# The last pair of neighbourhood attention heads asks for its scores amid its values' projection

## The chip, the cores and the metric

The kernel runs on one core of a Trainium2 chip. Its time is the device time of one execution in microseconds (us). TensorE (PE) does the matrix products and transposes, VectorE (DVE) and ScalarE (ACT) read its results from the eight PSUM banks and do the elementwise work, GpSimd (POOL) does some multiplications and copies, and SyncE (SP) issues most of the DMAs. The engines run side by side; each executes its own instructions strictly in the order in which they were written.

## The reference

Two encoder layers over 256 tokens and 16 meta tokens, with a model width of 2048. In each layer one projection feeds two groups of heads, gated linear attention (GLA) and neighbourhood attention (NA); their outputs, 16 blocks of 128 rows, go through one output projection. An MLP follows.

```
proj = jnp.einsum('bld,dp->blp', h, w_in)
gq, gk, gv, gr, glr, nq, nk, nv = jnp.split(proj, points, axis=-1)
y_gla = _gla_mixer(gq, gk, gv, gr, glr, gla_w_up, gla_b_up, gla_norm_w)
y_na = _na_mixer(nq, nk, nv, na_rel_bias).astype(h.dtype)
mix = jnp.einsum('blm,md->bld', jnp.concatenate([y_gla, y_na], axis=-1), w_out)
h = _layer_norm(DEEPNORM_ALPHA * h + mix, ln1_w, ln1_b)
```

NA has 16 heads of 64: a softmax over a window of the token grid with a learned bias, plus the meta tokens as keys. Only the first layer computes the meta tokens' own outputs.

```
s_loc = jnp.where(col_mask[:, :, None, :], s_loc + bias, -jnp.inf)
s_meta = jnp.einsum('bhnqd,bhmd->bhnqm', qb, km)
s = jnp.concatenate([s_loc.reshape(B, NA_HEADS, ncb, NA_QB, n_loc), s_meta], axis=-1)
p = jax.nn.softmax(s, axis=-1)
out = (jnp.einsum('bhnqrk,bhrnkd->bhnqd', p_loc, v_blk)
       + jnp.einsum('bhnqm,bhmd->bhnqd', p[..., n_loc:], vm))
```

## The kernel before

Each fp32 operand is split into a high and a low part (`wh`, `wl`; `x` likewise). A weight tile of 128x1024 is loaded by SyncE into one of three `raw` buffers (L192); ScalarE makes `wh` from it (L215) and VectorE `wl` (L216). So a load waits until the `wl` subtraction of the tile three before has been done. The tiles come in the order in which the matmuls use them, loaded some tiles ahead.

The NA heads are handled in pairs, 0 to 7. For each pair the projection (`by_m`) makes three blocks of columns: Q, K and V, here written Q7, K7, V7 for the last pair. A block is accumulated in one PSUM bank in two halves of 24 matmuls (L250, `eight`). `ev_na` takes a finished block out of its bank: for V that is a copy `nv` on ScalarE (L540), a copy `nr` of the meta columns on VectorE (L541), and two copies that complete `nr` on GpSimd (L544). When V is there, `ev_na` appends the generator `na_pair` to the list `fg`. Layer 0 has 272 columns (with the meta tokens); layer 1 has 256.

What a generator does between two `yield`s is one step. `pump` is called amid each block and at its end and runs one step of the first generator of `fg`; at the same places it may run steps of the GLA heads from `bg`, and a foreground step that was announced with `yield True` lets a waiting background step go on. The steps of a pair are:

1. the bias load `nb`, the output `na_out` of the pair two before (where more than one is due), the scores (L778, and L782 for the meta tokens in layer 0), and the softmax: adds `ns` (L787) and `nms` (L789), REDUCE (L754), the exps on ScalarE (L756), RECIPROCAL (L757), and the multiplications on GpSimd (L760), into `ns` and `npr`;
2. in layer 0, the softmax of the meta tokens (`nms`);
3. the stream transposes `nt` of the weights on VectorE (L799, L800);
4. `fetch` of the pair before (four DMAs `np` on SyncE, L826), the transposes of the values on TensorE (L805, L806, L808 for `nms`), their copies `v` (L811 on ScalarE, L812 on VectorE) and `npm` (L817), and the DMA `hop` (L819) that writes `nt` to memory, from where `fetch` will read it in another layout;
5. for pair 7 alone: `na_out(6)`, `fetch` of its own `np`, and `na_out(7)`, a step each.

`na_out` (L851, L858) multiplies `np` by `v` in two PSUM banks, and ScalarE and VectorE (L861, L862) take the result out as one block of `y`. There is one buffer for `np`.

After V7 comes the output projection `by_k`, over the 16 blocks of `y` two at a time: k = 0, 2, ..., 14. It accumulates four banks at once (L302 in layer 0; L312, `dense`, in layer 1), two from each of two pools. `mixed(k)` runs one `fg` step ahead of each k, and further ones if the blocks k and k + 1 aren't done; it also writes two additions `acc` (L424). Before the change, pair 7's steps fall so: scores at the end of V7, meta softmax at k=0, stream transposes at k=2, value transposes at k=4, `na_out(6)` at k=6, `fetch` at k=8, `na_out(7)` at k=10.

The order on each engine is that in which Python emits the instructions, with weight tiles ahead of their use and `issue_after` placing some DMAs behind named instructions. The pools pick the banks.

Of the kernel before, what the change touches and what calls it, by code (L numbers as in the profile page):

```python
# [58 lines left out]
class Trunk:  # L59
# [464 lines left out]
    def ev_na(self, j, ps):  # L524

        nc, m = self.nc, j % 3
        src = ps[:, :T].rearrange("p (r t w) -> p t r w", t=2, r=ROWS)
        if m == 0:
            t = self.a2.tile([P, L], F32, name="nq", tag="nq")
            nc.scalar.mul(t[:, NM:].rearrange("p (t r w) -> p t r w", t=2, r=ROWS), src, NAD ** -0.5)  # L530
            if self.full:
                nc.vector.tensor_scalar(t[:, :NM], ps[:, T:], NAD ** -0.5, None, ALU.mult)
            self.nqkv = [t]
            return
        if m == 1:
            t = self.a2.tile([P, 2, NKEY], F32, name="nk", tag="nk")
            own, rest = t[:, :, :P], t[:, :, P:]
        else:
            t = own, rest = self.nv[j // 3 % 2]
        nc.scalar.copy(own.rearrange("p t (r w) -> p t r w", r=ROWS), src)  # L540
        nc.vector.tensor_copy(rest[:, :, 32:NK2], ps[:, None, T:L].to_broadcast([P, 2, NM]))  # L541
        grid = lambda a: a.rearrange("p (r w) -> p r w", r=ROWS)
        for h, lo in ((0, 0), (1, 24)):
            nc.gpsimd.tensor_copy(grid(rest[:, h, :32]), grid(own[:, 1 - h, :])[:, :, lo:lo + 8])  # L544
        self.nqkv.append(t)
        if m == 2:
            self.y[8 + j // 3] = self.pair(self.yp, "y", 8 + j // 3)
            self.fg.append(self.na_pair(j // 3, *self.nqkv))
            self.wants[self.fg[-1]] = True

    def ev_r(self, c, ps):

# [206 lines left out]
            r = st[:, 2 * u:3 * u, None].to_broadcast(list(i.shape))  # L759
            by.tensor_tensor(o, i, r, ALU.mult)  # L760

    def na_pair(self, c, q, k, v):
        nc, b = self.nc, self.a2
        heads = [slice(hh * NAD, hh * NAD + NAD) for hh in range(2)]
        two = lambda a: a.rearrange("p (t c) -> p t c", t=2)
        bias = b.tile([P, 4, 192], F32, name="nb", tag="nb").rearrange("p u c -> p (u c)")[:, :4 * NKEY]
        bias = bias.rearrange("p (u c) -> p u c", u=4)
        nc.sync.dma_start(bias, self.i["nab"][self.l, c])
        s = b.tile([P, 4, NKEY], F32, name="ns", tag="ns", bufs=1)
        st = b.tile([P, 12], F32, name="nst", tag="nst")  # L770
        if len(self.due) > 1:
            self.due.popleft()()
        ps = self.spare(2)
        for t in range(2):
            for hh, hs in enumerate(heads):
                for part in heads:
                    at = NM + t * P + part.start
                    nc.tensor.matmul(ps[hh][part, t * NKEY:t * NKEY + NKEY], lhsT=q[hs, at:at + NAD], rhs=k[hs, t, :],  # L778
                                     start=True, stop=True)
        if self.full:  # L780
            for hh, hs in enumerate(heads):
                nc.tensor.matmul(ps[hh][:NAD, 2 * NKEY:2 * NKEY + NK2], lhsT=q[hs, :NAD], rhs=k[hs, 0, P:],  # L782
                                 start=True, stop=True)
            meta = self.nms
            sm = meta[:NM, :, :NK2]
        for hh in range(2):
            nc.vector.tensor_tensor(s[:, 2 * hh:2 * hh + 2, :], two(ps[hh][:, :2 * NKEY]), bias[:, 2 * hh:2 * hh + 2, :], ALU.add)  # L787
            if self.full:
                nc.vector.tensor_tensor(sm[:, hh, :], ps[hh][:NM, 2 * NKEY:2 * NKEY + NK2], self.qmask, ALU.add)  # L789
        pr = self.npr  # L790
        self.softmax(s, st, 4, ((s[:, :, :P], s[:, :, :P]), (pr[:, :, :NK2], s[:, :, P:])), nc.gpsimd)
        yield
        if self.full:
            mt = b.tile([NM, 6], F32, name="mst", tag="mst")
            self.softmax(sm, mt, 2, ((sm, sm),), nc.gpsimd)
        yield
        turned = b.tile([P, 4, 192], F32, name="nt", tag="nb")
        out = lambda at, n: turned[:, :, at:at + 32 * n].rearrange("p j (u c) -> p u j c", c=32)
        nc.vector.transpose(out(0, 4), s[:, :, :P])  # L799
        nc.vector.transpose(out(P, 2), pr.rearrange("p (h t) c -> p h (t c)", t=2))  # L800
        yield True
        self.fetch()
        pv = self.bank()
        for t in range(2):
            nc.tensor.transpose(pv[:, t * P:t * P + P], v[0][:, t, :], self.ident)  # L805
        nc.tensor.transpose(pv[:, T:T + P], v[1].rearrange("p t c -> p (t c)"), self.ident)  # L806
        if self.full:
            nc.tensor.transpose(pv[:, T + P:], meta.rearrange("p u c -> p (u c)"), self.ident)  # L808
        v1 = b.tile([P, 2, P], F32, name="v1", tag="v1")
        v2 = b.tile([P, P], F32, name="v2", tag="v2")  # L810
        nc.scalar.copy(v1, two(pv[:, :T]))  # L811
        nc.vector.tensor_copy(v2, pv[:, T:T + P])  # L812
        pm = None
        if self.full:
            pm = self.npm[c % 2]
            for hh, hs in enumerate(heads):
                nc.vector.tensor_copy(pm[hs, hh, :], pv[hs, T + P:T + P + NM])  # L817
        hop = self.hp.tile([P, 4, 192], F32, name="hop", tag="hop")
        nc.scalar.dma_start(hop, turned)  # L819
        p = []  # L820

        def fetch():
            p.append(b.tile([P, 4, 192], F32, name="np", tag="np", bufs=1))
            with self.tc.issue_after(self.asked):
                for j in range(4):
                    nc.sync.dma_start(p[0][32 * j:32 * j + 32], hop.rearrange("(i k) j c -> k i j c", i=4)[:, :, j])  # L826

        self.fetch = fetch
        self.due.append(lambda: self.na_out(c, v1, v2, p[0], pm))
        yield True  # L830
        if c == 7:
            self.due.popleft()()
            yield
            fetch()
            yield
            self.due.popleft()()
            yield
# [444 lines left out]
```

## Time and profile before

| | us |
|---|---|
| median of 3 runs | 2315.6 |
| the runs | 2315.4, 2315.6, 2317.69 |
| span of the profiled execution | 2314.3 |
| TensorE busy | 2300.4 |
| VectorE busy | 1519.4 |
| ScalarE busy | 1224.6 |
| GpSimd busy | 160.4 |

The profiled execution's own time is not listed apart from the runs; its span lies 1.3 us below their median, and 1.1 below the shortest of them. Times in the profile are microseconds from the span's start. The output projection begins at 331.8 in layer 0 and at 1505.0 in layer 1. A timeline row gives start, duration, engine, line, operation, output and inputs, shape, how many, and in brackets how long the engine stood idle before and what it was released by. A row of a TensorE wait gives what waited and for what, then the total, the number of times and the longest. The rows themselves are shown in the prediction.

### The profile page before, as it was taken

To read this page: it belongs to the slowest core of one execution; us is meant where nothing else is said; L and a number is where in the kernel's file an instruction comes from. 1 tells how busy PE (TensorE), PEld (TensorE's weight loads), DVE (VectorE), ACT (ScalarE), POOL (GpSimd) and SP (SyncE) were. 2 spreads that over 40 slices of the span, in tenths; PEclk is the share of its full clock that TensorE was granted. 3 is DMA by queue.
4 is the path that set the end of the run, shared out by engine and by line. 5 is a ranking of instruction groups with operands and counts; after the bars stand their busy time and mean duration, and the time that the engine had idled before them with its cause. 6 is when DMAs were issued, how large, how long until landed. Compare 5 with 4: busy or idle time off the path is not lost.

```text
span 2314.3 us, 45228 instructions
## 1 busy us (share of the span) xinstructions
PE 2300.4 (99%) x18420; PEld 2186.8 (94%) x18420; DVE 1519.4 (66%) x2392; ACT 1224.6 (53%) x2096; POOL 160.4 (7%) x245
## 2 busy tenths in 40 slices
PE   9999999999999999999999999999999999999998
PEld 9999999999999999999999899989988888888888
DVE  5588778875544455547576788788866455666654
ACT  5666665564433344444456766655654334555443
POOL 0023210100000000000020122200100000000000
PEclk9999999999999999999999999999999999999999
DMA  8556665555566666555555566666666666666664
GB/s 263 162 164 185 200 197 177 174 180 177 181 182 178 179 181 181 177 181 181 177 179 165 174 180 204 213 185 191 188 192 193 196 189 195 193 193 221 194 199 138
DMA packets 129824, 431.65 MB, mean 187 GB/s; under 512 B 14792, under 2 KB 23496, under 8 KB 129616
## 3 DMA queue, kind: packets, MB, share of 16 engines
q1 hardware_dynamic: 127024, 421.95, 60.1%
q10 hardware_dynamic: 2592, 6.82, 0.8%
q8 instruction: 144, 2.36, 0.4%
q14 instruction: 64, 0.52, 0.1%
HBM read 420.32 MB, written 8.39 MB: 185 GB/s over the span
## 4 chain that ended last, share of the span: by engine, by line
PE 79%; DVE 3%; ACT 1%; issue 1%; DMA 0%; POOL 0%; DVEq 0%; ACTq 0%; POOLq 0%; SPq 0%
PE mm L250 44%; PE mm L262 30%; PE mm L302 2%; PE mm L312 1%; DVE wl L216 1%; PE bg L312 0%; ACT wh L215 0%; PE bg L302 0%; DMA raw<-in_win 0%; DVE acc L1085 0%; PE bg L851 0%; DVE S L615 0%; ACT ns L756 0%; PE bg L983 0%; PE bg L470 0%
## 5 line engine op out<-in xcount | busy, mean ns | idle before, releaser
L216 DVE TENSOR_TENSOR wl<-raw,wh 128x1024 fp32r<-128x1024 f32 (+1 forms) x770 | 936.3, 1223 | 619.8 <-ACT wh L215 518.4
L215 ACT CAST wh<-raw 128x1024 fp32r<-128x1024 f32 (+1 forms) x770 | 805.4, 1048 | 753.2 <-PE mm L250 360.1
L250 PE MATMUL mm<-x,wh 128*128 128x272 f32 (+3 forms) x4544 | 805.3, 294 | 0.0
L250 PEld LDWEIGHTS mm<-x,wh 128*128 128x128 f32 x4544 | 646.8, 188 | 15.4 <-DVE gtn L577 0.3
L250 PE MATMUL mm<-x,wl 128*128 128x272 f32 (+3 forms) x2432 | 519.6, 284 | 0.0
L250 PEld LDWEIGHTS mm<-x,wl 128*128 128x128 f32 x2432 | 390.8, 188 | 0.0
L250 PE MATMUL mm<-y,wh 128*128 128x272 f32 (+1 forms) x1440 | 235.0, 285 | 0.0
L250 PEld LDWEIGHTS mm<-y,wh 128*128 128x128 f32 x1440 | 199.7, 188 | 0.1
L262 PE MATMUL mm<-x,wh 128*128 128x512 f32 x832 | 193.8, 390 | 0.0
L262 PEld LDWEIGHTS mm<-x,wh 128*128 128x128 f32 x832 | 154.3, 188 | 31.0
L250 PE MATMUL mm<-u,wh 128*128 128x272 f32 (+1 forms) x1056 | 172.1, 285 | 0.0
L262 PE MATMUL mm<-y,wh 128*128 128x512 f32 x688 | 162.2, 389 | 0.0
L262 PEld LDWEIGHTS mm<-y,wh 128*128 128x128 f32 x688 | 128.7, 188 | 26.5
L250 PE MATMUL mm<-y,wl 128*128 128x272 f32 (+1 forms) x720 | 146.4, 284 | 0.0
L250 PEld LDWEIGHTS mm<-u,wh 128*128 128x128 f32 x1056 | 146.3, 188 | 0.0
L262 PE MATMUL mm<-u,wh 128*128 128x512 f32 x496 | 118.3, 391 | 0.0
L250 PEld LDWEIGHTS mm<-y,wl 128*128 128x128 f32 x720 | 112.5, 188 | 0.0
L262 PEld LDWEIGHTS mm<-u,wh 128*128 128x128 f32 x496 | 90.9, 188 | 17.7
L250 PE MATMUL mm<-u,wl 128*128 128x272 f32 (+1 forms) x528 | 107.3, 284 | 0.0
L262 PEld LDWEIGHTS mm<-x,wl 128*128 128x128 f32 x832 | 98.4, 188 | 2.0
L262 PE MATMUL mm<-x,wl 128*128 128x256 f32 x832 | 98.8, 276 | 0.0
L262 PEld LDWEIGHTS mm<-y,wl 128*128 128x128 f32 x688 | 84.2, 188 | 2.8
(285 smaller groups left out, 2288.7 us busy)
## 6 DMA issues: line engine op xcount, KB each, us to landing
raw<-in_wff SPq DMA_DIRECT2D x512, 512.0 KB, 3.8
raw<-in_win SPq DMA_DIRECT2D x190, 512.0 KB, 4.3
raw<-in_wout SPq DMA_DIRECT2D x64, 512.0 KB, 4.2
hop<-nt ACTq DMA_DIRECT2D x16, 384.0 KB, 2.3
np<-hop SPq DMA_DIRECT2D x64, 96.0 KB, 4.6
nb<-in_nab SPq DMA_DIRECT2D x16, 352.0 KB, 4.9
xraw<-in_xT SPq DMA_DIRECT2D x7, 272.0 KB, 5.5
out<-out SPq DMA_DIRECT2D x5, 256.0 KB, 3.4
```

Source lines behind the costliest of these rows:

```text
L215: self.nc.scalar.copy(h, r)
L216: self.wl = self.nc.vector.tensor_tensor(lo, r, h.bitcast(F32), ALU.subtract).ins
L250: mm(o, lhsT=self.block(w, j), rhs=rhs, start=first and not i, stop=last and i == len(TURNS[once]) - 1)
L262: self.nc.tensor.matmul(o, lhsT=self.block(both[j // 8][low], j % 8), rhs=rhs, start=first and not i + j, stop=bool(last and i and j == 15 ...
L302: self.nc.tensor.matmul(ps[g + m][:, :n], lhsT=self.block(parts[p][0], 4 * j + m if first else 2 * m + j), rhs=acts[k + j][parts[p][1]][:, ...
L312: self.nc.tensor.matmul(o, lhsT=self.block(both[low], i), rhs=rhs, start=not low and k + i % 2 == 0, stop=k == DC - 2 and i % 2 == 1 and n ...
```

## The change

```diff
@@ ev_na @@
         if m == 2:
             self.y[8 + j // 3] = self.pair(self.yp, "y", 8 + j // 3)
-            self.fg.append(self.na_pair(j // 3, *self.nqkv))
-            self.wants[self.fg[-1]] = True
+        if m == (1 if j // 3 == 7 else 2):
+            self.fg.append(self.na_pair(j // 3, self.nqkv))
+            self.wants[self.fg[-1]] = m == 2
@@ na_pair @@
-    def na_pair(self, c, q, k, v):
-        nc, b = self.nc, self.a2
+    def na_pair(self, c, qkv):
+        nc, b, last = self.nc, self.a2, c == 7
+        q, k = qkv[:2]
+        if last:
+            yield True
...
         nc.vector.transpose(out(P, 2), pr.rearrange("p (h t) c -> p h (t c)", t=2))
+        if last:
+            yield
         yield True
         self.fetch()
+        v = qkv[2]
         pv = self.bank()
...
         yield True
-        if c == 7:
+        if last:
             self.due.popleft()()
             yield
             fetch()
```

Pair 7's generator is appended when K7 has been taken out of its bank, not V7. Its first step, at the end of K7, does nothing but wait for its turn. Its scores (with `na_out(5)` ahead of them) then come amid V7, its meta softmax at the end of V7, its stream transposes at k=0; the step at k=2 does nothing; and from the value transposes at k=4 on, the steps fall where they did. `v` is taken from the list when it is needed. This happens in both layers. No instruction is added or removed; below L547 lines move down by 1 to 7 (L760 becomes L761, L787 L791, L812 L819, L826 L833, L851 L858).

The order changes on all engines. GpSimd, layer 1, from the copies for K7 on (`nk` and `nr` are the pieces for K7 and V7, `ns` and `npr` the softmax's multiplications). Before:

```order
L544 COPY nk<-nk 128x32 x2
L544 COPY nr_16662<-nv_16661 128x32 x2
L760 TENSOR_TENSOR ns<-ns,nst 128x4x128
L760 TENSOR_TENSOR npr<-ns,nst 128x4x48
L1073 TENSOR_SCALAR acc<-acc,vec 128x256 x8
```

After:

```order
L544 COPY nk<-nk 128x32 x2
L761 TENSOR_TENSOR ns<-ns,nst 128x4x128
L761 TENSOR_TENSOR npr<-ns,nst 128x4x48
L544 COPY nr_16662<-nv_16661 128x32 x2
L1080 TENSOR_SCALAR acc<-acc,vec 128x256 x8
```

The copies that complete `nr` now stand behind the multiplications of the softmax. In layer 0 it is the same, with `nms` behind `nr`.

VectorE, layer 1, from pair 7's REDUCE or RECIPROCAL to the copy `v`. Before:

```order
L754 TENSOR_REDUCE nst<-ns 128x4
L424 TENSOR_TENSOR acc<-x_13298 128x256
L424 TENSOR_TENSOR acc<-x_13399 128x256
L216 TENSOR_TENSOR wl<-raw,wh 128x8x128
L424 TENSOR_TENSOR acc<-x_13531 128x256
L424 TENSOR_TENSOR acc<-x_13663 128x256
L757 RECIPROCAL nst<-nst 128x4
L799 STREAM_TRANSPOSE nt<-ns 128x4x4x32
L800 STREAM_TRANSPOSE nt<-npr 128x2x4x32
L216 TENSOR_TENSOR wl<-raw,wh 128x8x128
L812 COPY v_19184<-bg 128x128
```

After (REDUCE stands right ahead of the first row):

```order
L758 RECIPROCAL nst<-nst 128x4
L541 COPY nr_16662<-mm 128x2x16
L803 STREAM_TRANSPOSE nt<-ns 128x4x4x32
L804 STREAM_TRANSPOSE nt<-npr 128x2x4x32
L216 TENSOR_TENSOR wl<-raw,wh 128x8x128
L424 TENSOR_TENSOR acc<-x_13298 128x256
L424 TENSOR_TENSOR acc<-x_13399 128x256
L216 TENSOR_TENSOR wl<-raw,wh 128x8x128
L424 TENSOR_TENSOR acc<-x_13531 128x256
L424 TENSOR_TENSOR acc<-x_13663 128x256
L216 TENSOR_TENSOR wl<-raw,wh 128x8x128
L819 COPY v_19184<-bg 128x128
```

The eviction `nr` moves behind the RECIPROCAL, and three `wl` with two pairs of `acc` stand between the stream transposes and `v`, where one `wl` stood. In layer 0 it is the same, with `npm` behind `v`.

SyncE, layer 1, from the last weights of the projection to those of the output projection (`raw` are weight loads, `np` the four DMAs of a fetch, first pair 5's, then 6's and 7's, and `nb` pair 7's bias). Before:

```order
L826 DMA np<-hop 32x4x192 x4
L192 DMA raw<-in_wout 128x1024 x2
L768 DMA nb<-in_nab 128x704
L192 DMA raw<-in_wout 128x1024 x4
L826 DMA np<-hop 32x4x192 x4
L192 DMA raw<-in_wout 128x1024 x3
L826 DMA np<-hop 32x4x192 x4
```

After:

```order
L833 DMA np<-hop 32x4x192 x4
L192 DMA raw<-in_wout 128x1024 x2
L772 DMA nb<-in_nab 128x704
L192 DMA raw<-in_wout 128x1024 x3
L833 DMA np<-hop 32x4x192 x4
L192 DMA raw<-in_wout 128x1024 x5
L833 DMA np<-hop 32x4x192 x4
```

Of the loads around `np` of pair 6, one moves behind it, and one more stands ahead of `np` of pair 7. In layer 0 five and three loads become four and four.

The banks that the pools pick change with the order: the fourth bank of the output projection, which was V7's own in both layers, is now the bank of the first scores, which an addition of pair 7's softmax frees (`nms`, L793, in layer 0; the first `ns`, L791, in layer 1).

## The prediction

> **What bounds the kernel now.** I read the page's busy times first, then the windows around the two places that the change touches, then TensorE's waits there, and last the timeline of both places.
>
> ```profile
> span 2314.3 us, 45228 instructions
> PE 2300.4 (99%) x18420; PEld 2186.8 (94%) x18420; DVE 1519.4 (66%) x2392; ACT 1224.6 (53%) x2096; POOL 160.4 (7%) x245
> ...
> 332.00:345.00 13.00, 10.71 (x110) 10.31 (x110) 10.57 (x27) 7.74 (x28) 2.95 (x5) 1.00 0.71 205
> ...
> 1507.00:1520.00 13.00, 11.86 (x87) 10.12 (x88) 11.00 (x24) 7.72 (x24) 2.16 (x4) 1.00 0.75 209
> ...
> PE bg L808 <- POOL nms L760: 2.3, 1, 2.3
> ...
> PE mm L312 <- DVE nr L541: 0.9, 1, 0.9
> PE bg L851 <- DVE v L812: 0.6, 1, 0.6
> ```
>
> TensorE is busy for 99% of the span, so only what makes it stand still can be gained or lost. In the two windows, one for each layer (length, busy time of PE, PEld, DVE, ACT, POOL, then clock, DMA share, GB/s), PE is short of full by 2.29 and 1.14 us, while no other engine is full either: it stands still for single results. The wait rows say which: in layer 0 the transposes of pair 7's values wait 2.29 us for the meta weights `nms`; in layer 1 the output projection's fourth bank waits 0.90 us for the eviction of V7, and `na_out(6)` waits 0.56 us for the copy `v`. Together 3.75 us, 0.16% of the time: **all that the change could gain in these places**.
>
> **The change, layer 0.** No instruction is added or removed; the block of `na_out(5)` and pair 7's scores goes from the end of V7 to its middle.
>
> ```profile
> 329.31 0.65 PE L250 MATMUL mm<-x,wh 128*128 128x272 f32 x4
> ...
> 329.80 0.41 PE L250 MATMUL mm<-x,wl 128*128 128x272 f32 x2
> 330.12 0.79 DVE L424 TENSOR_TENSOR acc<-x 128x272 f32<-128x272 f32 x2
> 330.14 0.89 PE L851 MATMUL bg<-np,v 64*64 64x128 f32 x24
> ...
> 331.76 0.77 PE L302 MATMUL bg<-y,wh 128*128 128x272 f32 x4
> ...
> 332.42 1.15 POOL L544 COPY nr<-nv 128x32 f32<-128x32 f32 x2 [5.07 <-ACT nv L540]
> ...
> 333.26 0.18 DVE L541 COPY nr<-mm 128x32 f32<-128x32 f32 x1
> ...
> 335.93 0.88 DVE L754 TENSOR_REDUCE nst<-ns 128x4 f32<-128x704 f32 x1
> ...
> 337.76 0.38 PE L805 MATMUL bg<-ident,nv 128*128 128x128 f32 x2
> ...
> 339.07 1.04 POOL L760 TENSOR_TENSOR ns<-ns,nst 128x512 f32<-128x512 f32 x1 [5.51 <-DVE nst L757]
> ...
> 340.07 0.51 POOL L760 TENSOR_TENSOR npr<-ns,nst 128x192 f32<-128x192 f32 x1
> 340.14 0.71 DVE L799 STREAM_TRANSPOSE nt<-ns 128x512 f32<-128x512 f32 x1 [0.61 <-POOL ns L760]
> 340.53 0.34 POOL L760 TENSOR_TENSOR nms<-nms,mst 16x96 f32<-16x96 f32 x1
> 340.78 0.40 DVE L800 STREAM_TRANSPOSE nt<-npr 128x256 f32<-128x256 f32 x1
> 340.92 0.33 PE L808 MATMUL bg<-ident,nms 128*128 128x128 f32 x1 [2.29 <-POOL nms L760]
> 341.11 1.18 DVE L216 TENSOR_TENSOR wl<-raw,wh 128x1024 fp32r<-128x1024 f32 x1
> 342.21 0.28 DVE L812 COPY v<-bg 128x128 f32<-128x128 f32 x1
> 342.41 0.34 DVE L817 COPY npm<-bg 64x16 f32<-64x16 f32 x2
> ...
> 343.80 0.89 PE L851 MATMUL bg<-np,v 64*64 64x128 f32 x24
> ```
>
> Four projection matmuls go from 329.31 to 329.80, 0.123 us each; V7's second half has 24, so the block starts 2.95 us earlier, at about 327.2. It lasts 331.76 - 330.14 = 1.62 us, and the output projection still begins at 331.76: PE does the same work up to there. VectorE follows: from `nr` at 333.26 to the REDUCE at 335.93 it runs 2.67 us of work, which now, without `nr` (0.1), begins with the `acc` pair at 330.12. REDUCE starts at about 330.12 + 2.57 = 332.7, and GpSimd's `ns` 339.07 - 335.93 = 3.14 us behind it, at 335.8; I allow up to 336.3, as ScalarE has its exps amid other casts.
>
> GpSimd then does `ns` and `npr`, and only behind them the two `nr` copies that stood ahead of them (the order of GpSimd shows it): 335.8 + 1.00 + 0.46 + 1.15 = 338.4 to 338.9, and `nms` 0.3 later. The value transposes still come at 337.76 and reach `nr` at 338.0, so they wait 0.4 to 0.9 us for it, and 0.3 for `nms` right behind: **1.1 us in place of 2.29**.
>
> What is late next is the copy `v`. On VectorE three subtractions `wl` and two pairs of `acc`, where there was one `wl`, now stand between the stream transposes and `v`. The transposes end at about 335.8 + 1.04 + 0.1 + 1.1 = 338.0 to 338.5; 3 x 1.18 + 2 x 0.79 = 5.1 us later comes `v`, and with `npm` 0.54 more: 343.7 to 344.1. PE reaches `na_out(6)`'s second bank, which is the bank of the value transposes, at 343.80 - 1.2 + 0.2 = 342.8 (0.2 for what it does in the first bank): **a new wait of 0.9 to 1.3 us**. Layer 0 nets -2.29 + 1.1 + 1.1 = about 0, between -0.7 and +0.7.
>
> **The change, layer 1.**
>
> ```profile
> 1503.10 1.23 DVE L216 TENSOR_TENSOR wl<-raw,wh 128x1024 fp32r<-128x1024 f32 x1 [2.39 <-ACT wh L215]
> ...
> 1506.21 1.23 DVE L216 TENSOR_TENSOR wl<-raw,wh 128x1024 fp32r<-128x1024 f32 x1 [1.21 <-ACT wh L215]
> ...
> 1507.35 0.18 DVE L541 COPY nr<-mm 128x32 f32<-128x32 f32 x1
> ...
> 1508.98 0.88 DVE L754 TENSOR_REDUCE nst<-ns 128x4 f32<-128x704 f32 x1
> ...
> 1511.87 0.38 PE L805 MATMUL bg<-ident,nv 128*128 128x128 f32 x2
> ...
> 1512.46 1.04 ACT L215 CAST wh<-raw 128x1024 fp32r<-128x1024 f32 x1
> 1512.57 1.04 POOL L760 TENSOR_TENSOR ns<-ns,nst 128x512 f32<-128x512 f32 x1 [4.92 <-DVE nst L757]
> ...
> 1516.04 0.87 PE L851 MATMUL bg<-np,v 64*64 64x128 f32 x20 [0.56 <-DVE v L812]
> ...
> 1522.56 0.87 PE L851 MATMUL bg<-np,v 64*64 64x128 f32 x12
> ...
> 1507.46 8.68 SPq L192 DMA_DIRECT2D raw<-in_wout  x3
> 1517.08 1.75 SPq L826 DMA_DIRECT2D np<-hop  x4
> ...
> DMA to landing us min/median/max: 4.2/4.2/4.3
> ...
> DMA to landing us min/median/max: 3.5/3.9/4.8
> ```
>
> (The landing rows are those of `np` and of `raw`.) First, the fourth bank of the output projection is now a bank of the scores, freed by an add that ends near 1506, not V7's own bank: **0.90 us goes**, and the value transposes come at 1510.97 instead of 1511.87.
>
> Second, the `nr` copies. REDUCE now follows the subtraction that ends at 1504.33, behind what stood between `nr` and REDUCE (1.63 us) and two `acc` (0.76 by a pair's row of its kind, 0.79): 1506.6. `ns` came 1512.57 - 1508.98 = 3.59 us after REDUCE, but 0.5 of that was VectorE busy ahead of the reciprocal, which now follows REDUCE directly: 1509.7. With 1.00 + 0.46 + 1.15 `nr` is ready at 1512.3; PE asks for it at 1511.2. **A wait of 1.1 us**; by the ends, a start of `ns` between 1509.1 and 1510.4, it is 0.5 to 1.8.
>
> Third, `v`: the transposes end about 1511.9, three `wl` and two pairs of `acc` take 5.1 us, and `v` is there at 1517.2. PE, delayed by 1.1 - 0.9 = 0.2, asks for it at 1516.04 - 0.56 + 0.2 = 1515.7: a wait of 1.5 in place of 0.56, **+0.95 us** (0.4 to 1.4).
>
> Fourth, the queue of SyncE. A raw weight load waits until the subtraction of the tile three before it is done: the row at 1507.46 starts as the `wl` of 1506.21 ends. This `wl` now stands behind the softmax and the transposes and ends at about 1513.1, so its load goes out 5.6 us later; and one more load, a fifth, now stands ahead of the fetch `np(7)`. That fifth needs the tile which the late load brings: 1513.2 + 3.9 to land + 1.05 to cast + 1.23 to subtract = 1519.4, and `np(7)` goes out at 1519.5 rather than 1517.08. Its second piece, 0.45 later, lands 4.2 after that, at 1524.2; `na_out(7)` would ask at 1522.56 + 1.15 = 1523.7. **+0.5 to 1.1 us; I take 0.8**, with 0 and 1.8 as ends (loads landing in 3.5 or 4.8, and piece two or four the last one needed).
>
> Nothing is charged for `na_out(5)` and the scores in V7's middle: `nk`, which they read, is ready in layer 1 at 1500.0 by
>
> ```profile
> 1499.85 0.18 DVE L541 COPY nk<-mm 128x32 f32<-128x32 f32 x1
> ```
>
> and the scores come 1.5 us later; without that cover they would stall by what `nk` is late. The idle step issues nothing; it keeps the value transposes at k=4, where they were.
>
> **Sum.** Layer 0: 0. Layer 1: -0.90 + 1.1 + 0.95 + 0.8 = +1.95. The profiled span of 2314.3 becomes 2316.2; the median of the runs, 2315.6, lies 1.3 above that span, so I predict 2317.5 us.
>
> **The clock.** Both windows above show a clock of 1.00, the first with a stall of 2.29 us in it. The Trainium skill, "TensorE: Matmul & The Clock Gate", in its part on the HAM clock gate, says that TensorE falls to half its clock after an idle window of about 3.4 us and has to work as long to recover. The trace agrees as far as it goes, with full clock over a stall of 2.29 us. By that rule no wait of the forecast reaches the gate, and the sum stays.
>
> **Rivals.**
> - *All three old waits go and nothing comes.* For it: the softmax does end some 3 us earlier. Against it: the orders of GpSimd and VectorE put `nr` and `v` behind it. -3.75 us: 2311.9. Chance 0.10, with all between there and 2314.6.
> - *The waits only change their names.* If GpSimd's `ns` starts at the early ends and the fifth load lands in 3.5, layer 1 gives 0: -0.9 + 0.5 + 0.4 + 0. Time 2315.6, between 2314.6 and 2316.1. Chance 0.20.
> - *Slower: the fetch behind the fifth load.* If that load decides, each us by which `np(7)` leaves after about 1519.0 is a us on the path, since nothing but `na_out(7)` and the projection's last steps is left to put between. With the load landing in 4.8, ScalarE one cast of 1.04 behind, and the fourth piece needed, the term is 3.2 instead of 0.8; with the other terms at their upper ends (0.7; 1.8 - 0.9; 1.4) the sum is +6.2, 2321.8. It decides from a late load after about 1514. For it: ScalarE's casts do stand behind the exps. Chance 0.13, 0.10 of it above 2320.2.
> - *A stall so long that the clock falls.* From the rows this could begin anywhere above 2.29 us. If the third rival's wait of 3.2 us for `np(7)` made the next 3.2 us of matmuls run at half speed, it would cost as much again: 2325.0. Chance 0.02, as no row bears it out. By the figure of the Trainium skill, "TensorE: Matmul & The Clock Gate", part on the HAM clock gate, such a wait stays just short of the gate.
>
> That the change does not do what it says is excluded by the order of instructions: the scores do stand amid V7.
>
> **How the numbers follow.** The forecast, 2316.1 to 2319.1, has 0.55; with the others above that is all. The measurement can tell about 0.2%, 4.6 us. Faster by more than that needs more than all the waits there are: 0.03 of the first rival's 0.10, for what these views do not show. Slower by it is the upper part of the third rival and the fourth, 0.12; within, 0.85. The range, 2313.5 to 2320.3, takes in both ends of the unknown terms but not the first rival's full gain, nor the tops of the last two.
>
> **What would show it.** TensorE's waits in the profile after: the row on `nms` falls from 2.3 to below 1.3, with a part for `nr`; none on V7's eviction in layer 1; new rows on `v` or `npm` of about 1 in layer 0 and 1.5 in layer 1; SyncE's `np` at 1519 to 1520 and a wait of `na_out(7)` for it. The forecast is wrong if VectorE's subtractions do not hold up `v`, or if `np(7)` leaves as soon as `na_out(6)` is done.

## The result, and the profile after

| | before | changed |
|---|---|---|
| median of 21 runs each, us | 2317.45 | 2319.7 |
| ratio of changed to before, 95% interval | | 1.0013 [1.0007, 1.0019] |
| span of the profiled execution, us | 2314.3 | 2317.0 |

The change makes the kernel slower: by 0.13%, some 3 us, by the ratio, whose interval lies above 1; by 2.25 us between the medians; and by 2.7 us between the profiled spans. The 21 runs of before fall into five of 2314.7 to 2315.8 us and sixteen of 2317.1 to 2318.5 (the mean granted clock, on record for 33 later runs of it, is 1.000 in 12 that all took 2316.8 or less, and below that in all 16 above 2317.2), so its median depends on how many of each there are. The three runs that the prediction could see are among the 21, and their median lies 1.85 us below that of all. So the forecast time, 2317.5 us, is no more than the median of before, and it is the step of 1.9 us, forecast on top of the three, that is to be compared with the 2.25 to 3.0 measured. The range held the time.

The page's lines on span and busy times of the changed kernel:

```profile
span 2317.0 us, 45226 instructions
...
PE 2302.6 (99%) x18420; PEld 2188.1 (94%) x18420; DVE 1520.4 (66%) x2392; ACT 1224.1 (53%) x2096; POOL 157.9 (7%) x245
```

The view of TensorE's waits, in layer 0 and then in layer 1 (what waited and for what, total, times, longest):

```profile
PE bg L858 <- issue: 1.6, 1, 1.6
...
PE bg L858 <- DVE v L819: 1.8, 1, 1.8
PE bg L858 <- ACT x L337: 0.5, 1, 0.5
```

All three old waits are gone from these two places, and three new ones have come, each in `na_out` (L858): 1.63 us in layer 0, 1.78 in layer 1 for `v`, and 0.47 in layer 1, which the view puts down to a ScalarE operation that ended just then (more on it below). The waits hardly differ in sum, 3.88 us against 3.75. But TensorE is also *busy* 2.2 us longer, with the same 18420 matmuls. The windows of the changed kernel (length; busy time of PE, PEld, DVE, ACT, POOL; granted clock; DMA share; GB/s) show why:

```profile
332.00:345.00 13.00, 11.37 (x114) 10.83 (x113) 9.51 (x24) 7.54 (x23) 2.14 (x5) 1.00 0.55 155
1507.00:1520.00 13.00, 11.21 (x80) 9.43 (x79) 9.51 (x19) 7.85 (x23) 1.80 (x4) 0.90 0.54 169
...
1515.00:1516.60 1.60, 0.00 (x0) 0.00 (x0) 1.60 (x4) 0.33 (x2) 0.00 (x0) 1.00 0.83 248
1516.60:1518.00 1.40, 1.36 (x22) 1.10 (x23) 0.91 (x3) 1.33 (x4) 0.00 (x0) 0.75 0.83 260
1518.00:1519.00 1.00, 1.00 (x7) 1.00 (x7) 1.00 (x2) 0.17 (x1) 0.00 (x0) 0.50 0.97 217
1519.00:1520.00 1.00, 1.00 (x5) 0.90 (x5) 0.97 (x3) 0.39 (x2) 0.00 (x0) 0.50 0.73 299
1520.00:1521.00 1.00, 1.00 (x5) 0.76 (x4) 0.43 (x1) 0.40 (x1) 0.00 (x0) 0.65 1.04 246
1521.00:1522.00 1.00, 1.00 (x6) 0.83 (x5) 0.00 (x0) 0.00 (x0) 0.00 (x0) 1.00 0.80 242
```

In layer 1, 0.7 us after the stall's end, the granted clock falls to 0.50 and stays there until 1520.7, for 3.41 us (the trace has the two changes at 1517.29 and 1520.71). The timeline of both places (start, duration, engine, line, operation):

```profile
337.45 0.35 POOL L544 COPY nr<-nv 128x32 f32<-128x32 f32 x2
338.18 0.27 PE L813 MATMUL bg<-ident,nr 128*128 128x128 f32 x1
338.37 0.33 PE L815 MATMUL bg<-ident,nms 128*128 128x128 f32 x1
343.00 0.28 DVE L819 COPY v<-bg 128x128 f32<-128x128 f32 x1
343.65 0.76 PE L858 MATMUL bg<-np,v 64*64 64x128 f32 x18 [1.63 <-issue]
...
1511.00 0.35 POOL L544 COPY nr<-nv 128x32 f32<-128x32 f32 x2
1511.40 0.33 PE L813 MATMUL bg<-ident,nr 128*128 128x128 f32 x1
1516.30 0.29 DVE L819 COPY v<-bg 128x128 f32<-128x128 f32 x1
1516.64 0.96 PE L858 MATMUL bg<-np,v 64*64 64x128 f32 x20 [1.78 <-DVE v L819]
1517.53 1.22 PE L312 MATMUL bg<-y,wl 128*128 128x256 f32 x4
1518.55 1.05 PE L312 MATMUL mm<-y,wl 128*128 128x256 f32 x4
1519.49 2.37 SPq L833 DMA_DIRECT2D np<-hop  x4
1521.85 1.07 PE L312 MATMUL bg<-y,wh 128*128 128x512 f32 x4
1525.33 0.87 PE L858 MATMUL bg<-np,v 64*64 64x128 f32 x12 [0.47 <-ACT x L337]
```

The view of the tile `np` in the same stretch has the time from issue to landing of the fetch for pair 7:

```profile
DMA to landing us min/median/max: 5.3/5.4/5.5
```

Sixteen matmuls go from 1517.53 to 1521.85, 4.32 us. The same sixteen took 2.90 before:

```profile
1516.84 0.74 PE L312 MATMUL bg<-y,wl 128*128 128x256 f32 x4
...
1519.74 1.07 PE L312 MATMUL bg<-y,wh 128*128 128x512 f32 x4
```

So the slow clock costs 1.42 us, and 0.1 more in the `na_out` ahead of it: about 1.5. The second piece of `np(7)`, issued some 0.4 after 1519.49, has landed by 1525.19 in the trace, and `na_out(7)` starts 0.14 us later. In the second run below, where the view itself names the DMA, the same gap lies between the landing (1523.83) and the start (1523.97). So the wait of 0.47 is for this DMA, though the ScalarE operation ended at the same time; the first run below tests it.

To set layer against layer, count TensorE's instructions: the time from the 90th ahead of the output projection's first matmul to the projection's last, which are the same instructions in every kernel but the fifth run's. (This comes from the traces' TensorE records, matched by number.)

| us | layer 0 | layer 1 |
|---|---|---|
| before | 35.09 | 35.07 |
| changed | 34.95 | 37.39 |
| own `np` (run 1) | 36.37 | 36.02 |
| copies on ScalarE (run 2) | 34.62 | 39.09 |
| both (run 3) | 34.17 | 34.17 |
| no idle step (run 4) | 36.54 | 37.64 |
| own `np`, stall filled (run 5) | 34.63 | 34.79 |
| before, with both (run 6) | 35.08 | 34.51 |
| layer 0 alone (run 7) | 36.04 | 34.56 |

Within these two segments the loss of the change is all in layer 1: +2.32; layer 0 gives -0.14. That is 2.2 of the 2.7 us between the spans; the other 0.5 lies ahead of them and between them, in places that the change doesn't touch, and was not followed. Followed matmul by matmul, layer 1 stands at -1.22 against before when it has passed the fourth bank, at -0.99 behind the transpose of `nr`, at +0.23 behind the wait for `v` (1.78 for 0.56), at +1.75 behind the slow clock, at +2.40 behind the wait for `np`, and at +2.32 at its end.

### The profile page after: what moved, and what is told of

It reads as the page before. It is cut to its first block, busy times and chain, and to the rows that moved or that the text cites. A ratio compares the mean times of both kernels' runs of the same rounds, so it can differ in the third digit from the quotient of the medians.

```text
span 2317.0 us, 45226 instructions
## 1 busy us (share of the span) xinstructions
PE 2302.6 (99%) x18420; PEld 2188.1 (94%) x18420; DVE 1520.4 (66%) x2392; ACT 1224.1 (53%) x2096; POOL 157.9 (7%) x245
## 4 chain that ended last, share of the span: by engine, by line
PE 92%; DVE 4%; ACT 2%; issue 1%; POOL 1%; DMA 1%; DVEq 0%; SPq 0%; ACTq 0%; POOLq 0%
PE mm L250 53%; PE mm L262 30%; PE mm L302 3%; PE bg L302 1%; PE mm L312 1%; DVE wl L216 1%; DMA raw<-in_win 1%; ACT wh L215 1%; PE bg L858 1%; ACT ns L757 0%; PE bg L630 0%; DVE S L616 0%; PE bg L312 0%; PE bg L470 0%; PE mm L782 0%
```

## The experiments

Two theories on layer 1 were set against each other: that the wait for `v` with the slow clock, and the late fetch of `np(7)`, are two chains side by side which hide each other (A); or that the first is the whole loss (V, in the second run), or the second (B, in the first).

**Run 1: the fetch of pair 7 gets a buffer of its own** (that of the pair's bias, in place of the one that `na_out(6)` still reads).

```diff
-            p.append(b.tile([P, 4, 192], F32, name="np", tag="np", bufs=1))
+            p.append(b.tile([P, 4, 192], F32, name="np", tag="nb" if last else "np", **({} if last else {"bufs": 1})))
```

> The changed kernel with one edit: the fetch of pair 7 writes into the buffer of pair 7's bias, which is free by then, not into the one buffer of np that na_out(6) still reads. On SyncE it then stands behind three weight loads after the fetch of pair 6, as before the change, not behind five. Theory A (two chains side by side): in layer 1 the wait for v (1.78 us) with the half clock behind it ends at 1524.9, and the late fetch, issued at 1519.5 and landed 5.4 us later, at 1525.3; each hides the other. Then this edit alone takes only the last 0.47 us away: 2319.2, with the fetch issued near 1515 and landed by 1521, and the half clock after the wait for v as in the changed kernel. Theory B (the fetch alone sets the loss, and the clock falls because of something else): layer 1's whole loss of some 2.4 us goes, 2317.3. Theory C (the extra weight load ahead of the fetch is harmless): no change, 2319.7.

Measured: 2318.57 us, 1.0004 [0.9996, 1.0013]. The timeline of TensorE and SyncE in layer 1, then the landing of `np` there, then two windows with their clocks, one in each layer:

```profile
1517.88 1.00 PE L858 MATMUL bg<-np,v 64*64 64x128 f32 x20 [1.77 <-DVE v L819]
1525.92 0.89 PE L858 MATMUL bg<-np,v 64*64 64x128 f32 x24
...
1516.27 1.81 SPq L833 DMA_DIRECT2D np<-hop  x4
```

```profile
DMA to landing us min/median/max: 5.8/6.3/7.5
```

```profile
346.00:348.00 2.00, 2.00 (x12) 2.00 (x12) 1.85 (x5) 0.80 (x4) 0.00 (x0) 0.57 1.16 221
...
1519.00:1521.00 2.00, 2.00 (x9) 2.00 (x10) 2.00 (x4) 0.73 (x4) 0.00 (x0) 0.50 1.02 243
```

The fetch leaves at 1516.3, `na_out(7)` waits for nothing, and the stall for `v` and the half clock are as they were: what A says of this run, and against B. The time alone would not tell: 2319.2 (A) and 2317.3 (B) both lie within its interval. The gain in layer 1 is 1.37 us, more than the 0.47 expected. The rest is in the order: `na_out(7)` now runs in one piece of 24 matmuls (0.82 us until the next matmul starts, at 1526.74), where it had been two pieces of 12, one for each bank, which took 0.80 each (in the kernel before from 1522.56 to 1523.36). Layer 0, on the other hand, lost 1.4: there too the clock fell, to 0.57 in the window at 346, after a stall of 1.59, where the changed kernel had 1.63 and its profile stayed at 1.00.

**Run 2: the copies `v` and `npm` of pair 7 go to ScalarE.**

```diff
-        nc.vector.tensor_copy(v2, pv[:, T:T + P])
+        (nc.scalar.copy if last else nc.vector.tensor_copy)(v2, pv[:, T:T + P])
...
-                nc.vector.tensor_copy(pm[hs, hh, :], pv[hs, T + P:T + P + NM])
+                (nc.scalar.copy if last else nc.vector.tensor_copy)(pm[hs, hh, :], pv[hs, T + P:T + P + NM])
```

> The changed kernel with one edit: pair 7's copies v and npm, which stood on VectorE behind three subtractions of weights, are made by ScalarE right behind its own half of v. In layer 0 the wait of na_out(6) for them (1.63 us) goes, in layer 1 that of 1.78 us. Theory A (two chains): layer 0 gains 1.6; in layer 1 na_out(7) then waits for the fetch, which still leaves SyncE at about 1519 and lands near 1525, so almost nothing is gained there: 2318.1, with a wait of na_out(7) of 2.5 to 3 us. Theory V (the wait for v and the slow clock behind it are the loss, the fetch only the last 0.47): layer 0 gains 1.6 and layer 1 some 2.9: 2315.2. If the half clock is the answer to a TensorE stall in this stretch, it shows again behind the new wait, or not at all if there is none.

Measured: 2321.33 us, 1.002 [1.0011, 1.0029]: not faster than the change itself (the two intervals overlap), and 3 us above A's 2318.1. The timeline of TensorE and SyncE, then a window:

```profile
1513.72 0.87 PE L858 MATMUL bg<-np,v 64*64 64x128 f32 x20 [0.23 <-ACT v L819]
...
1523.97 0.87 PE L858 MATMUL bg<-np,v 64*64 64x128 f32 x12 [3.59 <-DMA np<-hop]
...
1517.94 1.75 SPq L833 DMA_DIRECT2D np<-hop  x4
```

```profile
1525.00:1527.00 2.00, 2.00 (x9) 1.90 (x10) 0.00 (x0) 0.00 (x0) 0.00 (x0) 0.50 0.48 190
```

The wait for `v` shrinks to 0.23, and TensorE then stands 3.59 us for the fetch, which still leaves behind five loads. V falls. What A's number had left out is the half clock: it moves with the stall, and comes behind the new one, not at 1518. So in the changed kernel the first stall and the slow clock had covered the late fetch; with the cover gone it costs more than they did (layer 1 at 39.09 for 37.39). In layer 0, 0.33 us was gained and not 1.6: `na_out(7)` waited twice there, 0.43 and 0.41 us, by the landings in the trace most likely for pieces of its fetch both times.

**Run 3: both edits.**

> The changed kernel with both edits of the two runs before: v and npm copied by ScalarE, and the fetch of pair 7 into a buffer of its own. Theory A: both chains are gone. Layer 0 keeps only the wait for nms of some 0.3 us where the kernel before had 2.29, layer 1 keeps some 0.2 where it had 0.90 and 0.56: about 3.3 us faster than the kernel before, 2314.1, and TensorE's clock stays at 1.00. Theory V: the same as the copies alone. A rival for all of these: that other waits come in their place further on (the output of na_out(6) on ScalarE, the fourth bank), then it ends near the kernel before, 2317.4.

Measured: 2314.39 us, 0.9987 [0.9978, 0.9996]: faster than the changed kernel and than the kernel before. TensorE's waits in layer 0, then in layer 1, and behind them a window:

```profile
PE bg L858 <- DVE acc L424: 0.8, 1, 0.8
...
PE bg L858 <- DVE acc L424: 0.7, 1, 0.7
...
PE bg L858 <- ACT v L819: 0.2, 1, 0.2
```

```profile
1519.00:1521.00 2.00, 1.89 (x15) 1.43 (x13) 1.44 (x2) 0.96 (x1) 0.00 (x0) 1.00 1.06 213
```

The wait for `v` is down to 0.2, the fetch stands behind three loads and not five, and the clock stays at 1.00. Of the 3.3 us expected some 2.6 came by the medians, 1.8 by the two layers' segments: a new wait of 0.7 to 0.8 us in each layer, at `na_out(7)`'s second bank, was not in the sum. The view names VectorE's `acc`, but the second bank also waits for the fetch's last two pieces. Layer 1's timeline, and the view of `np` there:

```profile
1521.59 0.87 PE L858 MATMUL bg<-np,v 64*64 64x128 f32 x20 [0.70 <-DVE acc L424]
...
L833 SPq DMA_DIRECT2D np<-hop x4: 383/422/432, 1513.8 to 1515.2; - x4
...
DMA to landing us min/median/max: 5.8/6.2/6.3
```

The last piece, issued at 1515.2, has landed by 1521.45, and `na_out(7)` goes on 0.14 us later, the gap of run 2; in layer 0 it is 349.62 and 349.75. So this is most likely what is left of the fetch's chain: it leaves early and takes 6 us. (In layer 1 an `acc` ends at the same moment, at 1521.56; no run took the two apart.)

**Run 4: no idle step.**

```diff
-        if last:
-            yield
         yield True
         self.fetch()
```

> The changed kernel without its idle step: the value transposes come at k=2, na_out(6) at k=4, the fetch at k=6 and na_out(7) at k=8. The copy v then stands behind one subtraction, not three, and the fetch behind three loads, not five. By the prediction's account of GpSimd, nr is ready 1.0 + 0.5 + 0.35 after the softmax's ns starts, at 337.8 in layer 0 and 1511.35 in layer 1, while TensorE asks at about 335.8 and 1509.2: a wait of some 2.2 us in each layer, nms with it in layer 0, and none for v or np. Against the kernel before: layer 0 2.3 - 2.29, about 0; layer 1 2.2 - 1.46 = +0.7, and up to 1.5 more if a stall of 2 us brings the half clock: 2318.1 to 2319.6. If the idle step is what costs (the chain to v and to the fetch begins one step late), it is nearer to 2317.

Measured: 2321.75 us, 1.0022 [1.0013, 1.003]. TensorE's timeline in layer 1, then a window:

```profile
1511.62 0.44 PE L810 MATMUL bg<-ident,nv 128*128 128x128 f32 x2 [1.20 <-ACT nv L540]
1513.52 0.33 PE L811 MATMUL bg<-ident,nr 128*128 128x128 f32 x1 [1.47 <-POOL nr L544]
```

```profile
1515.00:1517.00 2.00, 2.00 (x6) 1.52 (x6) 2.00 (x5) 0.39 (x2) 0.00 (x0) 0.50 0.88 237
```

In the profile the idle step is worth having, though the two intervals overlap: without it TensorE stalls twice on V7's pieces, 2.67 us in all (2.2 were expected), and the half clock follows. There is no wait for `v` or `np`, as said. The time is above the range expected, since layer 0 lost 1.45 too; 0.85 of it because `na_out(7)` ran there in two pieces, where it had been one.

**Run 5: run 1, with the stall filled.** Twelve matmuls that nobody reads, in layer 1 only:

```diff
             for i, ks in enumerate(heads):
+                if c == 6 and i and not turn and not self.full:
+                    spare = self.pm.tile([P, 512], F32, name="mm", tag="mm")
+                    for j in range(12):
+                        nc.tensor.matmul(spare[:, :T], lhsT=self.ones[D], rhs=self.x[j][0][:, :T], start=not j, stop=j == 11)
```

> The first run's kernel (the changed one, with pair 7's fetch in a buffer of its own), and in layer 1 twelve matmuls more, 128x256 into a spare bank that nobody reads, right where TensorE stood still for v: between the first four matmuls of na_out(6) and its second bank. They last 12 x 0.1155 = 1.4 us, so that of the wait of 1.77 us some 0.4 is left. If the stall brings the half clock (theory A): the clock stays at 1.00 from 1517 to 1523, v is there no earlier, and layer 1 is shorter than the first run's by the 1.5 us that the half clock cost, in spite of the added work: about 2317.0. If the clock falls for another reason (what TensorE does there, or power): it falls again, and nothing is gained: 2318.6. Layer 0 is as in the first run, with or without its own half clock (1.0 us).

Measured: 2316.78 us, 0.9995 [0.9986, 1.0005]. TensorE's timeline in layer 1, then two windows:

```profile
1514.03 1.63 PE L859 MATMUL mm<-x,ones 128*128 128x256 f32 x12
1515.87 0.87 PE L862 MATMUL bg<-np,v 64*64 64x128 f32 x20 [0.21 <-DVE v L819]
```

```profile
1517.00:1519.00 2.00, 2.00 (x14) 1.79 (x13) 1.61 (x3) 1.31 (x11) 0.00 (x0) 1.00 1.01 239
1519.00:1521.00 2.00, 2.00 (x11) 1.65 (x10) 0.94 (x3) 1.33 (x5) 0.00 (x0) 1.00 1.10 207
```

With TensorE at work through the stall, the clock stays at 1.00 and layer 1 is 1.23 us shorter than in run 1, with twelve matmuls more. So it is the standing still that brings the half clock here, and not the work that follows. (Layer 0, unchanged from run 1, had no half clock this time: 34.63.)

**Run 6: the kernel before, with both edits of run 3** (there `last` is `c == 7`).

> The kernel before with the two edits of the third run (v and npm of pair 7 copied by ScalarE, its fetch into the bias's buffer), and not the change: scores at the end of V7. If the third run is fast because of its edits alone, this one is as fast: 2314.4. If the early scores are worth what the prediction said of the waits that go: this kernel keeps the wait of 2.29 us for nms in layer 0 and of 0.90 for V7's bank in layer 1, loses that of 0.56 for v, and stands about 0.5 us below the kernel before, 2316.5, some 2 to 2.5 us above the third run.

Measured: 2315.2 us, 0.9994 [0.9985, 1.0003]. Its waits:

```profile
PE bg L808 <- POOL nms L760: 2.3, 1, 2.3
...
PE mm L312 <- DVE nr L541: 0.6, 1, 0.6
PE bg L851 <- DMA np<-hop: 0.6, 1, 0.6
```

The old waits for `nms` and V7's bank are there, and the early scores take them away: run 3's segments are 0.91 us shorter in layer 0 and 0.34 in layer 1, 1.25 together, not the 2 to 2.5 expected. The two intervals overlap, so that the timed runs alone do not tell run 3 from this one.

**Run 7: the change in layer 0 alone.**

> The change in layer 0 alone; layer 1 as in the kernel before. By the profiles' segment of layer 0 (from 90 matmuls ahead of the output projection to its end: 35.09 us before, 34.95 after) it is as fast as the kernel before, 2316.9, if the half clock doesn't come in layer 0, and up to 1.4 us slower where it comes, as it did in the first run (36.37). In layer 1 no half clock and no wait for np. If layer 0 carries part of the loss that was not seen in the profile, it is nearer to the changed kernel, 2319.

Measured: 2316.93 us, 0.9999 [0.999, 1.0008]. No loss can be seen, as expected, which fits a loss in layer 1; the interval only just overlaps that of the change. The profile has layer 0 at 36.04, without a half clock: pieces of `np(7)` came late, with a wait of 0.4 us and gaps in `na_out(7)`, a wait not expected there.

## Why the prediction came out as it did

The direction of the step was right, its size was 1.9 for 2.25 to 3.0, and of the chances the 0.85 for "within 0.2%" covers 0.13%, though the 21 runs of each kernel could tell this from no change, which the 0.2% had not allowed for. The time itself, 2319.7, lies above the forecast's own band, 2316.1 to 2319.1, in a stretch that had 0.03, the lower part of the third rival. That the step came near is luck: a wait of 1.1 us that hardly came stood against a clock that cost 1.5 us and had been put at nothing.

- **The base, 2315.6 us:** failed, by 1.85 us, as much as the step itself. It is a median of three runs, and the 21 have 2317.45. The 1.3 us between span and time was off as well: wherever both stand on record for one run, the time is 1.7 to 1.9 us above the span.
- **The fourth bank, -0.90:** right; measured -1.22, as a step shown by the position of the matmuls.
- **The wait for `nr`, 1.1 us in each layer:** failed. TensorE passed `nr` at 338.18 without a wait, and at 1511.40 with a step of 0.23. The step that failed is the price of GpSimd's copies, 1.15 us, taken from a row in which VectorE was subtracting weights at the same time (`wl`, from 332.12, in the row from 332.42). In the changed kernel they stand beside stream transposes and take 0.35. The two rows below, from the view of that line, hold all `nr` copies of a run, of the kernel before and then of the changed one, with the shortest, the median and the longest in ns: one copy takes from 0.2 to 1.2 us.

```profile
L544 POOL COPY nr<-nv x32: 203/306/1208, 179.4 to 1507.4; 128x32 f32<-128x32 f32 x32
```

```profile
L544 POOL COPY nr<-nv x32: 203/210/1227, 179.9 to 1511.1; 128x32 f32<-128x32 f32 x32
```

  The Trainium skill, "SBUF — State Buffer", section "Who interferes with whom", has the rule that the prediction passed over: a VectorE instruction with two SBUF inputs contends with a GpSimd instruction that reads SBUF, and the order of issue decides which of them is blocked. The trace agrees: of the 64 copies of this line in the kernel before, 21 took 0.99 us or more, each began while a subtraction `wl` (two SBUF inputs) ran and ended 0.07 us after it; 32 took 0.22 or less, and none of them began beside such a subtraction; the other 11 lie between. No run here was made to test it alone.
- **The wait for `v`:** mechanism right, shown by run 2. Sized 1.5 in layer 1 and 0.9 to 1.3 in layer 0, measured 1.78 and 1.63: `v` was copied some 0.2 to 0.6 us earlier than worked out, but TensorE, not held at `nr`, asked 0.8 earlier (342.0 and 1514.9).
- **The fetch of `np(7)`:** the queue was right to the digit, 1519.5. Two sizes were not: it landed in 5.4 us where 4.2 was taken, and TensorE came later, because of the clock. What was seen, 0.47, is near the 0.8 of the sum, but that is luck: it is the rest of a far larger delay, which with the first stall away (run 2) was 3.59 us. The third rival, priced at 3.2 for this wait, was nearer to the truth of the mechanism than the forecast.
- **The clock, 0 in the sum:** failed, by about 1.5 us, which is half of the loss or more. The step that failed is "no wait of the forecast reaches the gate": it rested on one stall of 2.29 us that had left the clock at 1.00, and the last section shows why that one said little. The Trainium skill, "TensorE: Matmul & The Clock Gate", on the HAM clock gate, asks for an idle window of about 3.4 us; here 1.78 us of standing still were enough, and run 5 shows that it was that. Where the page and the measurement differ, the measurement decides. The fourth rival had the mechanism, at a chance of 0.02 and behind a wait of 3.2 us only.
- **Layer 0, about 0:** -0.14 in the profile; the timed runs of layer 0 alone show no difference. Its terms were off as layer 1's: no wait for `nr`, and 1.63 for `v`.

## What to carry to other kernels

When a block is moved earlier, ask what had stood behind it on every queue: here the work that was passed (weight subtractions, loads) now stood ahead of the next consumer's copies and fetch, and the waits came back there. Two late chains can hide each other; removing one of them need not make a kernel faster, and each has to be judged with the other taken away. A stall of TensorE can cost almost twice its length (1.78 us and 1.5 more here), so fill it before counting it as small; and one profile in which a stall goes unpunished doesn't show that it is harmless. A releaser that a view names is the last one that it knows of; check the landings of the DMAs that the same instruction waits for.

## What the runs showed of the hardware that was not expected

The half clock came in layer 1 in every profile with a stall there of over 1.7 us (1.78, 1.77, 3.59) and in the one with two close together (1.20 and 1.47), began 0.6 to 1.0 us after the last stall's end, and lasted 3.41 us. It came in none with stalls of 0.8 or less. But in layer 0 a stall of 2.29 left the clock at 1.00 in the kernel before, one of 1.63 or 1.64 left it there in three profiles, and one of 1.59 did not.

The traces keep each change of the granted clock with its time, and in all nine the changes lie whole multiples of 3.413 us apart (in run 1: 6.39, 344.31, 347.72, 1518.50 and 1521.91 us, so 99, 1, 343 and 1 steps). So the clock seems to be set once in a step of 3.413 us, and where the steps lie in the kernel differs from execution to execution. With the steps laid over the stalls, their order becomes plain:

| run, layer | stall, us | step's boundary in it | most of it within one step, us | clock in the step after |
|---|---|---|---|---|
| run 2, layer 1 | 1520.38 to 1523.97 | 1521.42 | 2.55 | 0.50 |
| run 4, layer 1 | 1510.41 to 1511.62, 1512.06 to 1513.52 | 1511.15 | 1.94 | 0.50 |
| changed, layer 1 | 1514.86 to 1516.64 | none | 1.78 | 0.50 |
| run 1, layer 1 | 1516.11 to 1517.88 | none | 1.77 | 0.50 |
| before, layer 0 | 338.63 to 340.92 | 340.30 | 1.67 | 1.00 |
| run 6, layer 0 | 338.63 to 340.89 | 340.28 | 1.64 | 1.00 |
| run 1, layer 0 | 342.02 to 343.62 | none | 1.59 | 0.50 |
| run 5, layer 0 | 341.75 to 343.38 | 342.13 | 1.25 | 1.00 |
| run 7, layer 0 | 342.15 to 343.79 | 342.57 | 1.21 | 1.00 |
| changed, layer 0 | 342.01 to 343.65 | 343.11 | 1.09 | 1.00 |

(The idle times are the profile's, which models the ends of matmuls.) TensorE idle for 1.77 us or more of one step, about half of it, brought the half clock for the next step each time; 1.31 us or less (the most elsewhere in these traces) never did; between them 1.59 did and 1.64 and 1.67 did not, and what decides there is open. By this the stall of 2.29 us in the kernel before went unpunished because a boundary cut it, and it is luck, by where the steps lie, that the same stall in layer 0 is dear in run 1 and cheap in the changed kernel. In run 5 the step from 1512.90 to 1516.31 takes in the whole place of the filled stall, so without the twelve matmuls the clock should have fallen there too. The half clock may come in some executions of the kernel before too, but no profile shows it.

The fetch for pair 7 in layer 1 landed in 4.2 us (median) in the kernel before, and in 3.5 and 4.1 in runs 7 and 6, which have layer 1's scores where they were; with the early scores it took 4.9 to 6.3, as other loads moved with it. Which of them slowed it was not tried.
